# A masked-reconstruction loss: even columns to VectorE, odd ones to PE and ScalarE near the end, the target further forward in the stream, scales by pairs

One core of one Trainium2 chip. The metric is the device time of one execution in microseconds (us), least is best; the kernel before takes 77.78 us.

## The reference

```python
pred, target: (32, 147, 768) float32            # randn
mean = target.mean(-1, keepdims=True); var = target.var(-1, keepdims=True)
target = (target - mean) / np.sqrt(var + 1e-6)  # norm_pix_loss is True
loss = np.mean((pred - target) ** 2, axis=-1)
return loss.mean(axis=-1)                       # (32,)
```

## The kernel before

The 32 x 147 rows are laid on 128 partitions: each holds 36 or 37 rows, here called columns 0 to 36, of 768 elements (column 36, the rest, is on 96 partitions). `t` is target, `p` is pred. For each column VectorE makes mean and variance, ScalarE and VectorE the scale `r` and the negated mean `nm`, GpSimd the normalised column `s`. Then one of three ways: PE computes p - s into PSUM and ScalarE squares and sums it ("ACT"); VectorE takes the difference and ScalarE squares it ("DVE+ACT"); or VectorE does both ("DVE"). PE sums over partitions at the end, into `acc`.

```python
piece("t", 0, 4, q="hw"); piece("t", REST, REST + 1, q="hw")     # ... one statement a line in the kernel
...
piece("p", 4, 8)
piece("t", 20, 24)
piece("p", 8, 12)
piece("t", 24, 28)
piece("p", 12, 16)
piece("t", 28, 32)
piece("p", 16, 20)
piece("t", 32, 36)
...                                       # pred 20 to 31 by pairs, 32 to 34 singly, 35 in halves

def normalise(u, c):                      # GpSimd: reads the target tile in SBUF
    ...
    pin(nc.gpsimd.tensor_scalar(out=s[:n, so:so + D], in0=til[:n, o:o + D], scalar1=nm, scalar2=r,
                                op0=ALU.add, op1=ALU.mult))
def difference(u, d0, w):                 # VectorE: both inputs in SBUF
    ...
    pin(nc.vector.tensor_tensor(out=z[:, :w], in0=til[:, o:o + w], in1=s[:, so + d0:so + d0 + w],
                                op=ALU.subtract))
def square_dve(u, d0, w, dest):
    z = zs[u, d0][:, :w]
    pin(nc.vector.scalar_tensor_tensor(out=z, in0=z, scalar=1.0, in1=z, op0=ALU.mult, op1=ALU.mult,
                                       accum_out=dest))
...
finals.insert(0, ("rl_sum", rl_sum, mask, P))
for i, (need, vec, m, n) in enumerate(finals):   # PE: sums over partitions, [1, 32] each
    op(("final", i), "PE", 0.2, [need, "masks"], lambda v=vec, m=m, n=n: final(v, m, n), rank=90.0)
```

`op` lists an operation with an engine, a guessed duration and what it needs; a loop then sorts all of them by a simulated start time, and that is the program order on each engine. So each engine runs in a fixed order, and a change of one guess or need can move others.

## Time and profile before

| | before |
|---|---|
| time, median | 77.78 us (77.77 to 77.79) |
| profiled span | 76.0 us |
| busy: DMA row | full in slices 2 to 36 of 40 |
| busy: GpSimd, VectorE, ScalarE, PE | 71%, 69%, 41%, 39% of the span |
| HBM read | 28.90 MB, 380 GB/s over the span |

The shares of busy time average over the whole span; the end is set by what happens from 66 us on, which the prediction shows line by line.

### The profile page before, as it was taken

Reading aid. Unit: us, or ns where it says so; the run is one execution under the profiler, and the core shown is the slowest. Engines: PE = TensorE matmul, PEld = TensorE weight load, DVE = VectorE, ACT = ScalarE, POOL = GpSimd, SP = SyncE. Lnnn points to the kernel's source line nnn. Section 1 sums busy time; section 2 is a strip of 40 time slices with the busy share of each in tenths; the row PEclk is TensorE's granted clock in tenths of the full one; section 3 lists DMA queues with packets and bytes.
Section 4 is the critical chain, followed back from the end, with each engine's and each line's share of the span. In section 5 each row is a group of like instructions: output and inputs, shape, how many; then the busy total and the mean of one; then the engine's idle time right before and its main releaser. Section 6 shows DMA issues by size and latency. Waiting matters only on the chain.

```text
span 76.0 us, 535 instructions
## 1 busy us (share of the span) xinstructions
PE 29.5 (39%) x85; PEld 8.8 (12%) x86; DVE 52.3 (69%) x139; ACT 31.1 (41%) x61; POOL 54.0 (71%) x76
## 2 busy tenths in 40 slices
PE   0000000056898940679187708751642200004550
PEld 0000000011323300212031103110111000001020
DVE  0000499999999999927960896099429995499960
ACT  5100000400269501088019503940591669952960
POOL 4998205299998987598986898984488839994000
PEclk9999999999999999999965995699999555555555
DMA  0899999999999999999999999999999999999400
GB/s 0 213 420 310 251 228 236 210 220 213 210 217 217 213 214 217 217 210 213 217 217 217 213 215 217 210 220 210 220 199 212 210 215 210 216 200 201 61 0 0
DMA packets 3830, 15.41 MB, mean 203 GB/s; under 512 B 435, under 2 KB 1171, under 8 KB 3699
## 3 DMA queue, kind: packets, MB, share of 16 engines
q0 software_dynamic: 3568, 13.52, 88.2%
q1 hardware_dynamic: 258, 1.87, 6.8%
q14 instruction: 4, 0.02, 0.1%
HBM read 28.90 MB, written 0.00 MB: 380 GB/s over the span
## 4 chain that ended last, share of the span: by engine, by line
DMA 66%; DVE 21%; POOL 7%; issue 2%; PE 1%; ACT 0%; POOLq 0%; DVEq 0%; ACTq 0%
DMA t<-in_target_dram 49%; DMA p<-in_pred_dram 17%; DVE st L163 13%; POOL s L213 6%; DVE mv L164 3%; DVE zd L254 3%; DVE zd L249 2%; POOL p L113 1%; PE acc L307 1%; ACT r L187 0%; DVE r L193 0%; DVE ob L336 0%; POOLq L213 0%; DVEq L249 0%; ACTq L187 0%
## 5 line engine op out<-in xcount | busy, mean ns | idle before, releaser
L163 DVE BATCH_NORM_STATS2 st<-t 128x6 f32<-128x384 bf16 (+2 forms) x74 | 36.1, 530 | 14.2 <-DMA t<-in_target_dram 14.2
L213 POOL TENSOR_SCALAR s<-t,nm,r 128x768 bf16<-128x768 bf16 (+2 forms) x37 | 38.2, 1038 | 4.3 <-DVE r L193 2.2
L227 PE MATMUL z<-s,nident 128*128 128x512 bf16 (+3 forms) x36 | 13.8, 499 | 31.3 <-POOL s L213 26.9
L242 ACT ACTIVATE z<-z 128x1536 f32<-128x1536 f32 (+2 forms) x13 | 17.0, 1311 | 12.0 <-PE z L227 12.0
L227 PE MATMUL z<-p,ident 128*128 128x512 bf16 (+3 forms) x35 | 14.2, 548 | 12.2 <-DMA p<-in_pred_dram 12.0
L113 POOL DMA_DIRECT2D p<-in_pred_dram x17 | 9.6, 566 | 9.2 <-DMA t<-in_target_dram 4.3
L187 ACT ACTIVATE r<-mv,eps_t 128x4 f32<-128x4 f32 (+1 forms) x10 | 2.9, 293 | 26.8 <-DVE mv L164 26.1
L249 DVE TENSOR_TENSOR zd<-p,s 128x768 bf16<-128x768 bf16 (+1 forms) x9 | 7.3, 842 | 2.1 <-DMA p<-in_pred_dram 1.1
L242 ACT ACTIVATE zd<-zd 128x1536 bf16<-128x1536 bf16 (+1 forms) x6 | 7.6, 1264 | 2.8 <-DVE zd L249 2.8
L164 DVE BATCH_NORM_AGGREGATE mv<-st 128x2 f32<-128x12 f32 (+1 forms) x37 | 7.7, 209 | 1.3
L227 PEld LDWEIGHTS <-nident 128*128 128x128 bf16 (+1 forms) x37 | 3.4, 113 | 42.3 <-issue 23.0
L227 PEld LDWEIGHTS <-ident 128*128 128x128 bf16 (+1 forms) x37 | 4.8, 129 | 19.8 <-issue 18.5
L113 POOL DMA_DIRECT2D t<-in_target_dram x8 | 4.8, 622 | 1.0 <-POOLq L354 0.8
L193 DVE RECIPROCAL r<-r 128x4 f32<-128x4 f32 (+1 forms) x10 | 1.5, 148 | 2.8 <-ACT r L187 2.8
L254 DVE SCALAR_TENSOR_TENSOR zd<-zd 128x768 bf16<-128x768 bf16 x3 | 2.8, 949 | 0.0
L242 ACT ACTIVATION_READ_ACCUMULATOR z<-z 128x1 f32 (+1 forms) x13 | 2.4, 188 | 0.0
L188 ACT ACTIVATE nm<-mv 128x4 f32<-128x4 f32 (+1 forms) x10 | 1.9, 189 | 0.0
L187 ACT ACT_TABLE_LOAD x1 | 1.3, 1283 | 0.8 <-PEq L354 0.8
L307 PE MATMUL acc<-mask,rl 128*1 128x32 f32 x8 | 1.0, 229 | 0.7 <-ACT zd L242 0.4
L242 ACT ACTIVATION_READ_ACCUMULATOR zd<-zd 128x1 f32 x6 | 1.1, 186 | 0.0
L152 DVE MEMSET eps_t<- 128x1 f32 x1 | 0.1, 59 | 0.9 <-PEq L354 0.9
L307 PEld LDWEIGHTS acc<-mask,rl 128*1 128x1 f32 x8 | 0.4, 87 | 1.9 <-ACT zd L242 1.3
(25 smaller groups left out, 5.7 us busy)
## 6 DMA issues: line engine op xcount, KB each, us to landing
t<-in_target_dram POOLq DMA_DIRECT2D x8, 768.0 KB, 26.1
p<-in_pred_dram POOLq DMA_DIRECT2D x5, 768.0 KB, 26.4
p<-in_pred_dram POOLq DMA_DIRECT2D x6, 384.0 KB, 22.3
t<-in_target_dram SPq DMA_DIRECT2D x1, 1536.0 KB, 7.9
p<-in_pred_dram POOLq DMA_DIRECT2D x3, 192.0 KB, 12.8
t<-in_target_dram SPq DMA_DIRECT2D x1, 288.0 KB, 10.6
p<-in_pred_dram POOLq DMA_DIRECT2D x2, 96.0 KB, 9.8
p<-in_pred_dram POOLq DMA_DIRECT2D x1, 144.0 KB, 10.5
```

The source lines that it names most:

```text
L113: pin(eng.dma_start(out=til[:n], in_=src))
L163: pin(nc.vector.bn_stats(out=st[:n, j, :], in_=x))
L164: pin(nc.vector.bn_aggr(out=out, in_=st[:n, :len(parts)]))
L187: pin(nc.scalar.activation(out=r[:n], in_=mv[:n, :, 1], func=ACTF.Sqrt, bias=eps_t[:n], scale=1.0))
L188: pin(nc.scalar.activation(out=nm[:n], in_=mv[:n, :, 0], func=ACTF.Copy, scale=-1.0))
L193: pin(nc.vector.reciprocal(out=rs[g][:n], in_=rs[g][:n]))
L213: pin(nc.gpsimd.tensor_scalar(out=s[:n, so:so + D], in0=til[:n, o:o + D], scalar1=nm, scalar2=r, op0=ALU.add, op1=ALU.mult))
L227: pin(nc.tensor.matmul(z[:n, a:b], eye[:n, :n], src[:n, so + a:so + b], start=first, stop=not first))
L242: pin(nc.scalar.activation(out=z[:n, :w], in_=z[:n, :w], func=ACTF.Square, accum_out=dest[:n]))
L249: pin(nc.vector.tensor_tensor(out=z[:, :w], in0=til[:, o:o + w], in1=s[:, so + d0:so + d0 + w], op=ALU.subtract))
L254: pin(nc.vector.scalar_tensor_tensor(out=z, in0=z, scalar=1.0, in1=z, op0=ALU.mult, op1=ALU.mult, accum_out=dest))
L307: pin(nc.tensor.matmul(acc, vec[:n], m[:n], start=len(turn) == 1, stop=len(turn) == len(finals)))
```

## The change

Its intent: the statistics and normalised columns should be ready before their pred arrives, and from column 28 on VectorE (even columns) and PE with ScalarE (odd columns) should take turns, so that neither falls behind the stream.

```diff
     piece("t", 20, 24)
+    piece("t", 24, 28)
     piece("p", 8, 12)
-    piece("t", 24, 28)
+    piece("t", 28, 32)
     piece("p", 12, 16)
-    piece("t", 28, 32)
-    piece("p", 16, 20)
     piece("t", 32, 36)
-    for c in range(20, 24, 2):
-        piece("p", c, c + 2)
-    for c in range(24, 32, 2):
+    for c in range(16, 32, 2):
         piece("p", c, c + 2)
...
-    groups = [...] + [tuple(range(c, c + 4)) for c in range(4, KM, 4)]
-    units = [((c, c + 1), 0, D, "ACT" if c < 22 else "DVE+ACT") for c in range(0, KM - 4, 2)]
+    groups = [...] + [tuple(range(c, c + 4)) for c in range(4, 16, 4)]
+    groups += [(c, c + 1) for c in range(16, KM, 2)]
+    units = [((c, c + 1), 0, D, "ACT" if c < 18 else "DVE+ACT") for c in range(0, 24, 2)]
...
-    # 28 DVE, 29 DVE+ACT, (30, 31) DVE+ACT, 32 DVE, 33 DVE+ACT, 34 DVE   (summary of several lines)
+    units += [((24,), 0, D, "DVE"), ((25,), 0, D, "DVE+ACT"), ((26, 27), 0, D, "DVE+ACT")]
+    units += [((c,), 0, D, "ACT" if c % 2 else "DVE") for c in range(28, KM - 1)]
...
-    tail = 4
+    tail = 5
...
-    op("rl_sum", "DVE", 0.2, early_ops, lambda: pin(nc.vector.tensor_reduce(
-        out=rl_sum, in_=rl, axis=mybir.AxisListType.X, op=ALU.add)), rank=50.0)
+    def early_sum():
+        junk = singles.tile([P, n_early], F32, name="junk")
+        pin(nc.scalar.activation(out=junk, in_=rl, func=ACTF.Copy, accum_out=rl_sum))
+    op("rl_sum", "ACT", 0.4, early_ops, early_sum, rank=50.0)
```

The rest of the diff (a third queue that no piece uses, and the simulated start of ScalarE) adds no instruction. Columns 24 and 25, one pair before, become single columns, and VectorE now squares 24.

More of the change, by code (lines that the diff above doesn't have):

```diff
@@ L81 @@
     piece("p", KM - 1, KM, half, D)
-    groups = [tuple(range(0, 4)), (REST,)] + [tuple(range(c, c + 4)) for c in range(4, KM, 4)]
-    units = [((c, c + 1), 0, D, "ACT" if c < 22 else "DVE+ACT") for c in range(0, KM - 4, 2)]
+    groups = [tuple(range(0, 4)), (REST,)] + [tuple(range(c, c + 4)) for c in range(4, 16, 4)]
+    groups += [(c, c + 1) for c in range(16, KM, 2)]
+    units = [((c, c + 1), 0, D, "ACT" if c < 18 else "DVE+ACT") for c in range(0, 24, 2)]
     units.insert(2, ((REST,), 0, D, "ACT"))
-    units += [((KM - 4,), 0, D, "DVE"), ((KM - 3,), 0, D, "DVE+ACT"), ((KM - 2,), 0, D, "DVE"),
-              ((KM - 1,), 0, half, "ACT"), ((KM - 1,), half, D, "ACT")]
-    k = units.index(((KM - 8, KM - 7), 0, D, "DVE+ACT"))
-    units[k:k + 1] = [((KM - 8,), 0, D, "DVE"), ((KM - 7,), 0, D, "DVE+ACT")]
+    units += [((24,), 0, D, "DVE"), ((25,), 0, D, "DVE+ACT"), ((26, 27), 0, D, "DVE+ACT")]
+    units += [((c,), 0, D, "ACT" if c % 2 else "DVE") for c in range(28, KM - 1)]
+    units += [((KM - 1,), 0, half, "ACT"), ((KM - 1,), half, D, "ACT")]
     ops, by_name = [], {}
@@ L108, in load @@
         n, w = rows_of(c0), d1 - d0
-        til = data.tile([P, (c1 - c0) * w], F32 if q == "hw" else BF16, name=f"{kind}{c0}_{d0}")
+        til = data.tile([P, (c1 - c0) * w], BF16 if q == "sw" else F32, name=f"{kind}{c0}_{d0}")
         src = bass.AP(tensor=x.tensor, offset=x.offset + c0 * D + d0,
                       ap=[[N * D, B], [KJ * D, J - 1 if c0 == REST else J], [1, (c1 - c0) * w]])
-        eng = nc.sync if q == "hw" else nc.gpsimd
+        eng = {"hw": nc.sync, "hw2": nc.scalar, "sw": nc.gpsimd}[q]
         pin(eng.dma_start(out=til[:n], in_=src))
@@ L115, in load @@
             KIND[kind].setdefault(c, []).append((d0, d1, til, (c - c0) * w))
-    land, lanes, clock, last = {}, {"hw": [], "sw": []}, 2.9, {}
+    land, lanes, clock = {}, {"hw": [], "hw2": [], "sw": []}, 2.9
     for i, (kind, c0, c1, d0, d1, q) in enumerate(stream):
@@ L125 @@
         k = len(lanes[q])
-        op(("load", i), "SP" if q == "hw" else "POOL", 0.6, [], lambda a=stream[i]: load(*a), rank=-1.0,
+        op(("load", i), {"hw": "SP", "hw2": "ACT", "sw": "POOL"}[q], 0.6, [], lambda a=stream[i]: load(*a), rank=-1.0,
            early=0.0 if k <= 8 else lanes[q][k - 9] + 0.3)
@@ L314 @@
     free = {e: 0.0 for e in ("SP", "POOL", "DVE", "ACT", "PE")}
-    free["ACT"] = 2.1
+    free["ACT"] = 0.0
     end, left, order = {}, list(range(len(ops))), []
```

## The prediction

> **What bounds the kernel now.** I read the page first: the rows of 40 slices and the shares of the chain that ended last.
>
> ```profile
> DMA  0899999999999999999999999999999999999400
> GB/s 0 213 420 310 251 228 236 210 220 213 210 217 217 213 214 217 217 210 213 217 217 217 213 215 217 210 220 210 220 199 212 210 215 210 216 200 201 61 0 0
> DMA 66%; DVE 21%; POOL 7%; issue 2%; PE 1%; ACT 0%; POOLq 0%; DVEq 0%; ACTq 0%
> ```
>
> One slice is 1.9 us. The DMA row is full from slice 2 to slice 36, so for some 69 of the 76.0 us the queues had work without a gap. GB/s counts what is written, and most tiles are cast from f32 to bf16, so what is read is twice that, 28.90 MB in all. No engine sits above 71%. The stream is the bound, and the change removes no byte from it. All that is open to a change of order and of engines is the part after the stream, so the second view is the timeline of the last 13 us (start, length, engine, line, operation):
>
> ```profile
> 63.01 6.18 POOL L213 TENSOR_SCALAR s<-t,nm,r 128x768 bf16<-128x768 bf16 x4
> 66.22 1.41 DVE L249 TENSOR_TENSOR zd<-p,s 128x768 bf16<-128x768 bf16 x2 [1.11 <-DMA p<-in_pred_dram]
> 67.56 0.94 DVE L254 SCALAR_TENSOR_TENSOR zd<-zd 128x768 bf16<-128x768 bf16 x1
> 68.44 2.50 DVE L249 TENSOR_TENSOR zd<-p,s 128x1536 bf16<-128x1536 bf16 x3
> 70.86 0.94 DVE L254 SCALAR_TENSOR_TENSOR zd<-zd 128x768 bf16<-128x768 bf16 x1
> 71.12 0.48 PE L227 MATMUL z<-p,ident 128*128 128x384 bf16 x1 [1.08 <-DMA p<-in_pred_dram]
> ...
> 71.62 0.48 PE L227 MATMUL z_last<-p,ident 128*128 128x384 bf16 x1
> 71.73 0.08 DVE L254 DVE_READ_ACCUMULATOR zd<-zd 128x1 f32 x1
> 71.73 0.55 DVE L249 TENSOR_TENSOR zd<-p,s 128x768 bf16<-128x768 bf16 x1
> ...
> 72.32 0.96 DVE L254 SCALAR_TENSOR_TENSOR zd<-zd 128x768 bf16<-128x768 bf16 x1
> 72.34 0.47 ACT L242 ACTIVATE z<-z 128x384 f32<-128x384 f32 x1
> ...
> 72.84 0.47 ACT L242 ACTIVATE z_last<-z_last 128x384 f32<-128x384 f32 x1
> ...
> 73.20 0.17 DVE L300 TENSOR_REDUCE rl_sum<-rl 128x1 f32<-128x18 f32 x1
> ...
> 73.85 0.18 DVE L336 COPY ob<-acc 1x32 f32<-1x32 f32 x1 [0.49 <-PE acc L307]
> ```
>
> The two halves of the last column reach PE at 71.12 and 71.62, which I take as their landings. VectorE has no gap from 66.22 to 73.37: it enters the last 5 us behind the stream. Its columns 32 and 34 land before the last column, yet their squares end at 71.8 and 73.28. ScalarE, kept busy by the squares that follow VectorE's differences, takes up the first half at 72.34, though PE was done with it at about 71.60. Both engines end at about 73.4, so 1.8 us lie between the last landing and the last square. From there to `ob` it is 0.4 us, and 2.15 us more to the end of the span. The third view, the groups by shape in 61 to 76 us (busy us, mean ns), shows why VectorE is late:
>
> ```profile
> L213 POOL TENSOR_SCALAR s<-t,nm,r 128x768 bf16<-128x768 bf16 x4 | 6.2, 1557 | 0.0
> L249 DVE TENSOR_TENSOR zd<-p,s 128x1536 bf16<-128x1536 bf16 x4 | 4.4, 1112 | 1.0 <-POOL s L213 0.9
> L254 DVE SCALAR_TENSOR_TENSOR zd<-zd 128x768 bf16<-128x768 bf16 x3 | 2.8, 949 | 0.0
> ```
>
> GpSimd's last four normalisations take 1557 ns each, where the median of all 37 is 976 and the longest 2452; VectorE's longest difference of two columns takes 1561 ns where the median of the nine differences of either width is 919. Both are slow only while the other runs.
>
> **What the Trainium skill says.** "SBUF — State Buffer", Who interferes with whom: a VectorE instruction with two SBUF inputs contends with a GpSimd instruction that reads SBUF, and the later one waits for all of the earlier. The stretched pairs above agree. "VectorE: DVE Perf Modes", The perf-mode tier table: a bf16 `tensor_tensor` runs at twice the plain rate and has no faster form. The trace agrees as far as it goes: 0.55 us for 768 elements, 0.92 for 1536, against 0.95 for the `scalar_tensor_tensor` over 768. So a column's square costs VectorE far more than its difference. "DMA: Bandwidth & Descriptors", Bandwidth, gives rates for whole transfers; none is needed here, as this trace has the rate.
>
> **The change part by part.**
>
> *Engines from column 28 on.* VectorE before, from 28 to 34, counted from column 28's arrival: 1.41 (differences 28, 29), 0.95 with its accumulator read (square 28), 2.50 (differences of 30 with 31, 32 and 33, one of them stretched), 0.95, 0.55, 0.96, with small overlaps 66.22 to 73.28, 7.06 us. After: columns 28, 30, 32 and 34 alone, each a difference of 0.55 and a square with read of about 1.0, 4 x 1.55 = 6.2 us. From 66.2 that is 72.4 at the earliest. The stream sets no later end: taking a column as about 0.93 us of stream (the last landings before show that pace), pair 30 lands at about 67.7, column 32 at 68.7, and 34 at 70.6. VectorE then squares 30 by 69.3, 32 by 70.85 and 34 by 72.4. This saves 0.9 us there, of which 0.6 is the stretch that goes with GpSimd's late normalisations, the rest the three differences of odd columns less one square.
>
> ScalarE: odd columns need PE's two products (about 0.75 us after landing at the half clock that the trace grants from 58 us on) and a square of 768. I put that at 0.84, as for `zd`, plus 0.19 for the read, 0.95 with overlap. Column 31: landing 67.7, PE 68.5, square to 69.45. Column 33: landing about 69.6, PE 70.4, square to 71.4. So ScalarE is free when PE has the first half at 71.6: squares 71.65 to 72.2 and 72.2 to 72.75. Before, they were the same two instructions from 72.34 to 73.43, 1.09 us. They start 0.7 us earlier, no longer behind VectorE's backlog.
>
> *Target further forward.* In the listing of the stream, target pieces 24, 28 and 32 each move past one piece of four pred columns, so each lands 3.66 us sooner (the waits of `bn_stats` on target, at 41.96, 49.28 and 56.61, put eight columns at 7.32 us). Target 32 lands at 52.95 and its statistics take 4.6 us, to 57.6, where before they ended at 61.2. The last normalisations can then end by about 62, not 69.2, far before VectorE's tail. This removes the stretch from the tail; it takes nothing from the stream.
>
> *Scales by pairs.* From column 16 on, ten pairs in place of five groups of four: five more each of square root (0.29), negated mean (0.19) and reciprocal (0.15). That is 2.4 us on ScalarE and 0.75 on VectorE, all before 59 us, where VectorE waits some 2 us for each target piece. Cost on the path: nothing. Gain: GpSimd starts a pair 2.3 us sooner, also off the path.
>
> *Columns 18 to 21 to VectorE.* Two more differences of 1536, 1.84 us, at 57.6 to 60. VectorE catches up by the time pair 22 lands at about 60.3 and pair 24 at 62.2; these can still be stretched by GpSimd.
>
> *Early sums by ScalarE.* The `tensor_reduce` of 0.17 at 73.20 goes; ScalarE's sum of about 0.4 us falls between squares 31 and 33, at 69.5 to 69.9, where it waits only for pred. The path loses a reduction that sat on the end of VectorE; some of it was beside ScalarE's last square.
>
> *Pieces.* One pred piece of four columns (16 to 19) becomes two. One more issue of 0.55 on GpSimd, and perhaps 0.04 of stream.
>
> Sum: the path is last landing 71.6 (unchanged), PE 0.48, square and read to 72.75, then as before 0.4 to `ob` at 73.15 in place of 73.85. **Minus 0.7 us**, span 75.3. The timed median is 1.78 above the profiled span before, so 77.1.
>
> **The rivals.** *A: PE's order gives it back.* The listing of instructions shows PE taking the sums of columns into `acc` in between: the last half's product stands behind the sum of column 33, which needs ScalarE's square at 71.4, only 0.2 before the last landing. The subtraction for the last column's first half stands behind the square of 31. If PE or ScalarE is 0.4 late there, the tail is 0.3 to 0.4 longer: 77.4 to 77.5. For it: the granted clock of 0.5 and three engines in a ring. Against it: the slack above.
>
> *B: the stream gets longer.* GpSimd issues in order and an issue waits for the landing eight back, so a normalisation that waits for a pair's reciprocal, behind a square waiting for a later pred, could hold an issue. Then 0.3 to 1 us more, 77.4 to 78.5. Against: I followed each late issue through the order; the last needs pair 24's landing at 62.2, as before, 8 us ahead of its data.
>
> *C: the stream gets shorter.* From 66 us on the rate was 194 to 215 GB/s against a steady 215. If GpSimd's and VectorE's collisions cause that, their removal gives up to 0.3 us: 76.8. Against it: small pieces at the end explain it as well, and these stay. A gain of 2% needs 1.56 us, nearly the whole 1.8 us behind the last landing; I see no way to it.
>
> **Range and chances.** The middle is 77.1. C alone gives 76.8, A gives 77.5, and a mild B lies within; 76.75 to 77.5 should hold it 8 times in 10. Within 2% (76.22 to 79.34): 0.94. Faster than that needs stream and tail together: 0.04. Slower needs a hard form of B: 0.02.
>
> **What would show it.** Right: PE takes the last half at 71.5 to 71.7; ScalarE takes the first half within 0.1 us of PE's end; VectorE's last square ends near 72.4 and ScalarE's at 72.75; the last four normalisations end before 63; differences of 768 stay near 0.55; `ob` near 73.15. Wrong: the last landing moves by over 0.3 us (B or C); PE's last product starts later than its landing (A); a DMA share under 0.9 in any slice to 36; VectorE still without a gap at 72.5.

## The result

Ratios here and below are the mean time of one kernel's fast runs over the mean of the kernel before's in the same rounds, so not quite the ratio of the medians quoted beside them.

The changed kernel takes 77.25 us (77.17 to 77.32, six runs) against 77.80 in the same rounds: a ratio of 0.993 (0.9917 to 0.9943), and 0.55 us faster. The span went from 76.0 to 75.6 us. The page of the changed kernel, the same rows as before:

```profile
DMA  0799999999999999999999999999999999999700
GB/s 0 208 416 315 252 231 229 224 221 208 208 211 218 215 219 218 221 208 208 211 218 218 212 218 224 208 211 202 216 211 211 211 211 213 211 203 206 107 0 0
DMA 60%; DVE 18%; POOL 9%; issue 6%; PE 2%; ACT 1%; POOLq 0%; ACTq 0%
```

The stream is as full and as long as before; its last slice with data holds 107 GB/s in place of 61 because each slice is now 75.6/40 us. So nothing came from the transfers. The timeline of the changed kernel's tail (start, length, engine, line, operation, and in brackets the idle time ahead and who ended it) answers to the one in the prediction:

```profile
69.66 0.48 PE L224 MATMUL z<-s,nident 128*128 128x384 bf16 x1 [0.17 <-ACT z L239]
...
69.93 0.84 PE L224 MATMUL z<-p,ident 128*128 128x512 bf16 x2
...
70.81 0.80 ACT L239 ACTIVATE z<-z 128x768 f32<-128x768 f32 x1 [0.86 <-PE z L224]
...
71.22 0.48 PE L224 MATMUL z<-p,ident 128*128 128x384 bf16 x1 [0.26 <-DMA p<-in_pred_dram]
71.48 0.96 DVE L251 SCALAR_TENSOR_TENSOR zd<-zd 128x768 bf16<-128x768 bf16 x1
...
71.63 0.40 PE L307 MATMUL acc<-mask,rl 128*1 128x32 f32 x4
71.74 0.47 ACT L239 ACTIVATE z<-z 128x384 f32<-128x384 f32 x1
...
71.96 0.50 PE L224 MATMUL z_last<-p,ident 128*128 128x384 bf16 x1
...
72.50 0.47 ACT L239 ACTIVATE z_last<-z_last 128x384 f32<-128x384 f32 x1 [0.18 <-PE z_last L224]
...
73.44 0.18 DVE L336 COPY ob<-acc 1x32 f32<-1x32 f32 x1 [0.99 <-PE acc L307]
```

VectorE's last square now runs from 71.48 to 72.45, where it ended at 73.28. ScalarE takes the first half at 71.74, not at 72.34. `ob` comes at 73.44, not at 73.85, though the first half landed 0.1 us later in this trace (71.22 against 71.12, where PE stood idle for it). A measure free of that shift is the **tail**: from the start of the first half's pred product to `ob`. It was 73.85 - 71.12 = 2.73 us and is 2.22. That 0.5 is the gain.

Not all went well: the last half's product starts at 71.96, though in the kernel before it followed the first half's by 0.5 us (71.62 behind 71.12), so that the data should be there at about 71.7. Just ahead of it in PE's order stand four passes of sums (from 71.63): two for column 32, and two for column 33, and these two need ScalarE's square of 33, ended at 71.71. And GpSimd is later than I had reckoned. Here are its last normalisations, and VectorE's first difference, in order of time:

```profile
57.57 1.94 POOL L210 TENSOR_SCALAR s<-t,nm,r 128x768 bf16<-128x768 bf16 x2
57.62 2.69 DVE L246 TENSOR_TENSOR zd<-p,s 128x1536 bf16<-128x1536 bf16 x1
...
60.61 2.28 POOL L210 TENSOR_SCALAR s<-t,nm,r 128x768 bf16<-128x768 bf16 x1 [0.59 <-DVE r L190]
...
63.45 1.95 POOL L210 TENSOR_SCALAR s<-t,nm,r 128x768 bf16<-128x768 bf16 x1
```

A difference that takes 0.92 us alone lasted 2.69 us beside two normalisations, and held back the reciprocal behind it; the last two normalisations then stretched to 2.28 and 1.95 us. They end at 65.4 us, not at 62, but still ahead of the tail.

### The profile page after: what moved, and what is told of

Same layout as the page of the kernel before. It is cut to its first block, busy times and chain, and to the rows that moved or that the text cites. A ratio compares the mean times of both kernels' runs of the same rounds, so it can differ in the third digit from the quotient of the medians.

```text
span 75.6 us, 570 instructions
## 1 busy us (share of the span) xinstructions
PE 30.1 (40%) x87; PEld 8.9 (12%) x88; DVE 56.4 (75%) x148; ACT 32.0 (42%) x73; POOL 54.5 (72%) x77
## 2 busy tenths in 40 slices
DMA packets 3973, 15.41 MB, mean 204 GB/s; under 512 B 450, under 2 KB 1186, under 8 KB 3842
## 3 DMA queue, kind: packets, MB, share of 16 engines
HBM read 28.90 MB, written 0.00 MB: 382 GB/s over the span
## 4 chain that ended last, share of the span: by engine, by line
DMA 60%; DVE 18%; POOL 9%; issue 6%; PE 2%; ACT 1%; POOLq 0%; ACTq 0%
DMA t<-in_target_dram 49%; DVE st L160 13%; DMA p<-in_pred_dram 11%; POOL s L210 8%; DVE mv L161 3%; DVE zd L246 1%; PE acc L307 1%; POOL t L110 1%; PE z L224 1%; ACT z_last L239 1%; PE z_last L224 1%; POOLq L368 0%; DVE r L190 0%; POOL p L110 0%; DVE ob L336 0%
## 5 line engine op out<-in xcount | busy, mean ns | idle before, releaser
L224 PE MATMUL z<-s,nident 128*128 128x512 bf16 (+4 forms) x36 | 13.8, 493 | 23.1 <-POOL s L210 17.2
L239 ACT ACTIVATE z<-z 128x1536 f32<-128x1536 f32 (+3 forms) x14 | 16.6, 1184 | 7.6 <-PE z L224 7.3
L224 PE MATMUL z<-p,ident 128*128 128x512 bf16 (+4 forms) x35 | 14.8, 558 | 12.6 <-DMA p<-in_pred_dram 12.3
L184 ACT ACTIVATE r<-mv,eps_t 128x2 f32<-128x2 f32 (+2 forms) x15 | 4.4, 293 | 29.7 <-DVE mv L161 28.9
L110 POOL DMA_DIRECT2D p<-in_pred_dram x18 | 10.2, 566 | 3.2 <-DMA p<-in_pred_dram 2.2
L246 DVE TENSOR_TENSOR zd<-p,s 128x768 bf16<-128x768 bf16 (+1 forms) x10 | 9.7, 991 | 0.5 <-ACT zd L239 0.3
L239 ACT ACTIVATE zd<-zd 128x1536 bf16<-128x1536 bf16 (+1 forms) x5 | 6.7, 1346 | 2.7 <-DVE zd L246 2.7
L251 DVE SCALAR_TENSOR_TENSOR zd<-zd 128x768 bf16<-128x768 bf16 x5 | 4.8, 955 | 0.1
L190 DVE RECIPROCAL r<-r 128x2 f32<-128x2 f32 (+2 forms) x15 | 1.9, 124 | 2.2 <-ACT r L184 2.2
L185 ACT ACTIVATE nm<-mv 128x2 f32<-128x2 f32 (+2 forms) x15 | 2.8, 189 | 0.0
```

What stands on the lines that cost most here:

```text
L110: pin(eng.dma_start(out=til[:n], in_=src))
L184: pin(nc.scalar.activation(out=r[:n], in_=mv[:n, :, 1], func=ACTF.Sqrt, bias=eps_t[:n], scale=1.0))
L185: pin(nc.scalar.activation(out=nm[:n], in_=mv[:n, :, 0], func=ACTF.Copy, scale=-1.0))
L190: pin(nc.vector.reciprocal(out=rs[g][:n], in_=rs[g][:n]))
L224: pin(nc.tensor.matmul(z[:n, a:b], eye[:n, :n], src[:n, so + a:so + b], start=first, stop=not first))
L239: pin(nc.scalar.activation(out=z[:n, :w], in_=z[:n, :w], func=ACTF.Square, accum_out=dest[:n]))
```

## The experiments

The question is which part of the change brought the 0.5 us. **Theory E**: the swap of engines, which takes the odd columns off VectorE. **Theory C**: the order of the stream, which ends GpSimd's normalisations before VectorE's tail, so that the two no longer stretch each other. The prediction counted both in its 0.9 us for VectorE and divided them only by reckoning. All experiments gave correct results and were timed in five rounds, with four to six runs kept of each.

| run | median us | ratio to before (95%) | tail us |
|---|---|---|---|
| before | 77.7 to 77.8 | 1 | 2.73 |
| changed | 77.25 | 0.993 (0.9917 to 0.9943) | 2.22 |
| only_engines | 77.59 | 0.9987 (0.9974 to 1.0) | 2.70 |
| only_stream | 77.11 | 0.9932 (0.992 to 0.9944) | 2.12 |
| undo_engines | 77.13 | 0.9931 (0.9918 to 0.9945) | 2.15 |
| undo_stream | 78.36 | 1.0084 (1.0071 to 1.0096) | late start |
| undo_pairs | 77.99 | 1.0019 (1.0002 to 1.0037) | late start |
| undo_sum | 77.29 | 0.9943 (0.9931 to 0.9955) | 2.28 |
| extra_reads | 79.26 | 1.0202 (1.018 to 1.0224) | 4.10 |
| extra_writes | 77.24 | 0.994 (0.9928 to 0.9953) | 2.13 |
| sums_last | 77.02 | 0.9908 (0.9896 to 0.9921) | 1.96 |
| pe_order | 76.93 | 0.9903 (0.9889 to 0.9918) | 1.95 |
| pe_split | 77.27 | 0.9942 (0.9928 to 0.9955) | 2.04 |
| old_engines_sum | 77.15 | 0.9926 (0.9912 to 0.9939) | 2.11 |

"Late start" means that PE took the first half well after it landed, so the measure does not hold there. In pe_split the first piece is larger and lands later.

### One part alone, and the change without it

**only_engines**: the kernel before with

```diff
+    units += [((c,), 0, D, "ACT" if c % 2 else "DVE") for c in range(28, KM - 1)]
```

in place of its units from 28 to 34.

> The kernel before, with only the engines of columns 28 to 35 as in the changed kernel (even ones VectorE alone, odd ones PE and ScalarE). Theory E (the swap of engines does it: VectorE has 4 x 1.55 us in place of 7.06): 77.3 to 77.4, VectorE's last square at about 72.4 to 72.7. Theory C (the gain is the normalisations leaving the tail, so VectorE's two-input instructions are no longer stretched): the last normalisations still run to about 69 us and still stretch a difference, and the odd columns now wait for them on PE; 77.7 to 77.9, with a normalisation or a difference of over 1.5 us after 66 us.

At 77.59 us it lies in neither range, and is 0.1 us under the kernel before, at the edge of noise. The trace has the sign that was named for C: normalisations still ran past 66 us (to 67.97), and VectorE's square of 28 took 1.63 us and its difference 0.82. VectorE's last square ended at 73.19, hardly sooner than before. Its timeline:

```profile
62.96 5.01 POOL L209 TENSOR_SCALAR s<-t,nm,r 128x768 bf16<-128x768 bf16 x4
...
66.29 0.82 DVE L245 TENSOR_TENSOR zd<-p,s 128x768 bf16<-128x768 bf16 x1 [1.24 <-DMA p<-in_pred_dram]
...
67.15 1.63 DVE L250 SCALAR_TENSOR_TENSOR zd<-zd 128x768 bf16<-128x768 bf16 x1
```

**only_stream**: the kernel before with only the new order of pieces.

```diff
+    piece("t", 24, 28)
     piece("p", 8, 12)
...
+    for c in range(16, 32, 2):
```

> The kernel before, with only the order of the stream as in the changed kernel (target pieces 24, 28, 32 earlier, pred 16 to 19 as two pieces). Theory E: VectorE still has the differences of 29, 31, 33 in its tail; 77.6 to 77.8. Theory C: normalisations end by 63 us, the two-column difference of 30 and 31 falls from 1.56 to 0.95 us, VectorE's last square ends at about 72.7 in place of 73.3; 77.2 to 77.4.

This has the whole gain, 0.57 us (77.11, below both ranges), and a shorter tail than the changed kernel. The difference of columns 30 and 31 fell from 1.56 to 0.96 us. VectorE's last square ended at 72.68 in place of 73.28, and these 0.60 us are the size of the gain:

```profile
71.72 0.96 DVE L251 SCALAR_TENSOR_TENSOR zd<-zd 128x768 bf16<-128x768 bf16 x1
```

These are its groups by shape in 66 to 76 us (busy us, mean ns):

```profile
L251 DVE SCALAR_TENSOR_TENSOR zd<-zd 128x768 bf16<-128x768 bf16 x3 | 2.9, 951 | 0.0
...
L210 POOL TENSOR_SCALAR s<-t,nm,r 128x768 bf16<-128x768 bf16 x1 | 1.3, 1288 | 0.1
L246 DVE TENSOR_TENSOR zd<-p,s 128x1536 bf16<-128x1536 bf16 x1 | 1.0, 959 | 0.1
```

The one normalisation that reaches into the window began at 64.89 and was over by 66.2, later than the 63 that I expected.

**undo_engines**: the changed kernel with columns 28 to 34 on the engines of before.

> The changed kernel, with columns 28 to 34 on the engines of the kernel before. Theory E: gives the gain back, 77.6 to 77.8. Theory C: keeps most of it, 77.3 to 77.45, because the early sum on ScalarE and the early normalisations stay.

Taking the swap back costs nothing: 77.13, below both ranges and at the same ratio as the changed kernel. Theory E falls as the source of the gain. This kernel still has the early sum on ScalarE, the scales by pairs and the new engines of columns 18 to 21, 24 and 25, and only_stream has none of these. The two ratios are 0.9931 and 0.9932, so with the old engines from column 28 on, these parts together bring nothing that can be told from noise.

**undo_stream**: the changed kernel with the old order of pieces.

> The changed kernel, with the stream's order of the kernel before. Theory E: 77.3 to 77.4. Theory C: normalisations end near 69 us again, and hold PE's subtraction of columns 33 and 35; 77.6 to 77.9.

All of the change but the stream is slower than the kernel before, by 0.84%, beyond what C expected. The last two normalisations began at 64.27 and took 5.10 us together, beside VectorE's own work:

```profile
63.98 3.83 DVE L249 TENSOR_TENSOR zd<-p,s 128x1536 bf16<-128x1536 bf16 x5
...
64.27 5.10 POOL L213 TENSOR_SCALAR s<-t,nm,r 128x768 bf16<-128x768 bf16 x2 [0.59 <-DVE r L193]
...
69.42 0.48 PE L227 MATMUL z_last<-s,nident 128*128 128x384 bf16 x1 [2.60 <-POOL s L213]
69.69 0.84 PE L227 MATMUL z<-p,ident 128*128 128x512 bf16 x2
```

The harm comes through PE's order: the subtraction for the last half needs the last normalised column and stands in PE's order ahead of column 31's product. PE waited 2.60 us for it while column 31's pred lay ready, as the product took off at once behind it. The swap by itself does not do this: only_engines has the same order on PE, but its normalisations ended at 67.97, not at 69.37, PE waited 0.98 us, and it was no slower than the kernel before. Which of the other parts made the normalisations later no run separates.

### The contention by itself

**extra_reads**: only_stream with four normalisations into a tile that nobody reads, behind GpSimd's last needed one. They add no need to any other engine, so what is put back is only GpSimd's reading of SBUF beside VectorE.

```diff
+    def extra():
+        x = singles.tile([P, 2 * D], BF16, name="x")
+        for j in range(4):
+            til, r = tbuf[KM - 1][0][2], rs[KM - 1]
+            pin(nc.gpsimd.tensor_scalar(out=x[:, 0:D], in0=til[:, j * D:(j + 1) * D], scalar1=r[1], scalar2=r[0],
+                                        op0=ALU.add, op1=ALU.mult))
+    op("extra", "POOL", 4.0, [("norm", KM - 1)], extra, rank=80.0)
```

> The stream-order-only kernel (77.11) with four more normalisations into a scratch tile, nobody's input, at the end of GpSimd's order, so that they run from 66 us on beside VectorE's tail as the needed ones did in the kernel before. Contention theory: some of VectorE's instructions of 0.55 and 0.95 us there stretch to 1.0 us and more, and the time is 0.3 to 0.8 us longer, 77.4 to 77.9. Rival (the gain was in having the normalised columns sooner, not in a free port): unchanged, 77.05 to 77.2.

79.26 us: 2.1 us more than only_stream, and well over the upper end of what I expected. Each of VectorE's three squares in the tail took 1.5 to 1.6 us (two are shown):

```profile
65.97 7.88 POOL L301 TENSOR_SCALAR x<-t,nm,r 128x768 bf16<-128x768 bf16 x4
...
66.94 1.57 DVE L251 SCALAR_TENSOR_TENSOR zd<-zd 128x768 bf16<-128x768 bf16 x1
...
73.11 1.54 DVE L251 SCALAR_TENSOR_TENSOR zd<-zd 128x768 bf16<-128x768 bf16 x1
```

This shows the mechanism and not its size. The extra normalisations run to 73.85, where the needed ones of the kernel before ended at 69.19; there the differences were stretched (1.41 and 2.50 us above) and the squares kept 0.94 us.

**extra_writes**: the control, with six memsets of 768 bf16 in the same place.

```diff
-            pin(nc.gpsimd.tensor_scalar(...))
+            pin(nc.gpsimd.memset(x[:, 0:D], 0.0))
+            if j < 2:
+                pin(nc.gpsimd.memset(x[:, D:2 * D], 0.0))
```

> The control to extra_reads: six memsets of 768 bf16 in the same place, which write SBUF and read nothing. Contention over the reading side only: VectorE's instructions keep 0.55 and 0.95 us and the time stays at 77.05 to 77.2. If any GpSimd work in the tail costs: 77.3 or more.

77.24 us, 0.04 above the range given, with an interval that overlaps only_stream's and the same tail within 0.01 us. The square that runs beside memsets kept its 0.95 us; the other two come after the last memset, which ended at 70.29. The differences beside them took 1.03 and 1.43 us, where only_stream has 1.08 and 1.43:

```profile
66.73 0.73 POOL L302 MEMSET x<- 128x768 bf16 x1
67.03 0.95 DVE L251 SCALAR_TENSOR_TENSOR zd<-zd 128x768 bf16<-128x768 bf16 x1
```

So GpSimd's normalisations, which read SBUF, stretch VectorE's instructions with two inputs, and are stretched in turn (1.56 to 2.33 us each in extra_reads, 0.98 alone); GpSimd's being busy is not enough. VectorE's instructions with one input show nothing of it: the 74 `bn_stats` of the kernel before, many of them beside normalisations, took 503 to 562 ns. Theory C is shown: the mechanism by these two runs, its size by only_stream.

### The other parts

**undo_pairs**: the changed kernel with

```diff
-    groups = [...] + [tuple(range(c, c + 4)) for c in range(4, 16, 4)]
-    groups += [(c, c + 1) for c in range(16, KM, 2)]
+    groups = [...] + [tuple(range(c, c + 4)) for c in range(4, KM, 4)]
```

> The changed kernel with scales of columns 16 to 35 by fours again. Theory: off the path; the last normalisations end at 66 to 68 us in place of 65.4, if that reaches past 66 us one square of VectorE stretches by 0.3 to 0.6 us, and VectorE has slack of 0.3 only: 77.2 to 77.6. Rival: pairs cost VectorE and ScalarE time that shows: 77.0 to 77.15.

77.99 us (77.64 to 78.05, a wide scatter), over the range given, and no faster than the kernel before. The normalisation of 32 waits for the statistics of all four columns and starts at 59.73, not 57.57; the last ends at 67.45, not 65.4. That stretches the square of 28, as expected, and does what I had not seen: PE's subtraction for the last half, which needs that last column, holds the products of 29 and 31 behind it.

```profile
66.71 1.54 DVE L250 SCALAR_TENSOR_TENSOR zd<-zd 128x768 bf16<-128x768 bf16 x1
67.50 0.48 PE L223 MATMUL z_last<-s,nident 128*128 128x384 bf16 x1 [8.04 <-POOL s L209]
...
67.77 1.49 PE L223 MATMUL z<-p,ident 128*128 128x512 bf16 x4
```

In the changed kernel the product of 29 started at 66.01. So beside the rest of the change the pairs are needful, where only_stream, with scales by fours as well, is at 77.11. The trace points to the swap, which puts 29 and 31 on PE; no run has fours with the swap and the new stream alone.

**undo_sum**: the early sum on VectorE again, by a `tensor_reduce` at the end of its order.

> The changed kernel with the early sum by VectorE again, at the end of its order. VectorE ends at 72.45 + 0.17 = 72.62, ScalarE's last square at 73.08, so the sum is hidden: 77.2 to 77.3. Rival: it sits on the path: 77.35 to 77.45.

77.29, hidden: VectorE made the sum at 72.42, while ScalarE's last square was still to come (72.61).

### PE's order

**sums_last**: the changed kernel, with every sum but the first two needing (in the sorting only) the last product.

```diff
-    op(("final", i), "PE", 0.2, [need, "masks"], lambda ...)
+    op(("final", i), "PE", 0.2, [need, "masks"] + ([("pred", len(units) - 1)] if i > 1 else []), lambda ...)
```

> One half of pe_order: only the sums of columns 32 and 33 go behind the last half's product; the subtraction for the last column's first half still stands ahead of column 33's pred product. If the place of the sums is the whole loss: 76.9 to 77.0, as pe_order. If the subtraction's place matters as much, ScalarE still ends column 33 at 71.7 and takes the first half at 71.75: 77.0 to 77.15.

77.02 us: the last product started 0.50 us behind the first half's and `ob` came 0.26 us sooner. The place of the sums is nearly the whole loss. By the ratios it is 0.17 us, and the intervals just touch; the tails, one trace of each, say 0.26.

```profile
71.72 0.48 PE L224 MATMUL z_last<-p,ident 128*128 128x384 bf16 x1
```

**pe_order**: the same, and the subtraction for the last column's first half behind column 33's product.

```diff
-    ... + ["ident"],
+    ... + ["ident"] + ([("pred", k - 2)] if (u, d0) == ((KM - 1,), 0) else []),
```

> The changed kernel with PE's order alone altered: column 33's pred product ahead of the subtraction for the last column's first half, and the sums of columns 32 and 33 behind the last half's product. Theory Q (the changed kernel loses 0.3 us in PE's queue: the last half, landed by about 71.65, is taken up at 71.96): the last product starts within 0.1 us of its landing, 0.2 to 0.35 us faster than the changed kernel measured 77.25, so 76.9 to 77.05. Rival: VectorE's square of column 34 ends at 72.45 and ScalarE is as full as PE, so nothing is gained: 77.2 to 77.3.

76.93 us, the fastest of all, 0.32 us under the changed kernel's median (0.21 us by the ratios, each taken against the kernel before in its own rounds). The second step is not told apart from sums_last (0.9903 and 0.9908, tails 1.95 and 1.96). PE in its tail:

```profile
71.13 0.48 PE L224 MATMUL z<-p,ident 128*128 128x384 bf16 x1
71.62 0.48 PE L224 MATMUL z_last<-p,ident 128*128 128x384 bf16 x1
72.03 1.01 PE L307 MATMUL acc<-mask,rl 128*1 128x32 f32 x10
```

**pe_split**: pe_order, with the last column cut at 512 in place of 384.

> As pe_order, and the last column is cut at 512 of 768 in place of 384. Theory Q with a shorter last piece: its product and its square are over a third shorter, 0.15 us less than pe_order, 76.75 to 76.95, unless VectorE's square of 34 (72.45) or the first piece's longer square then ends last: no change against pe_order.

A miss: 77.27. The first piece reached PE 0.26 us later than in pe_order's trace and its product and square are longer, so ScalarE took it up at 72.00 and began the last at 72.59, where pe_order's began at 72.14. Of the two cuts tried, equal halves are the better: there ScalarE begins the last square as soon as it has done with the first.

**old_engines_sum**: undo_engines, with ScalarE's early sum moved ahead of its last two squares, to see whether the swap is worth something once PE's order is good.

```diff
-    op(("sq", k), "ACT", ..., [("pred", k)], ...)
+    op(("sq", k), "ACT", ..., [("pred", k)] + (["rl_sum"] if u == (KM - 1,) else []), ...)
```

> undo_engines (ratio 0.9931) with ScalarE's early sum moved from behind the last square to ahead of the last column's two squares; PE's order there has no sum ahead of the last product. Theory: the swap of engines is worth something only where PE's order is good: this kernel loses 0.13 to 0.2 us against undo_engines and still ends with VectorE's square of 34 at 72.6, so 77.0, above pe_order (ratio 0.9903) by under 0.1. Rival: the swap is worth nothing or less: equal to pe_order or faster, a ratio of 0.990 or under.

77.15, not 77.0, a miss: the tail is 2.11 against undo_engines' 2.15, because VectorE's square of 34 ended at 72.85 and three sums came after it. pe_order's tail is 0.16 shorter, with that square ended at 72.35. The intervals of the two ratios overlap slightly (0.9889 to 0.9918, 0.9912 to 0.9939), so where nothing waits in PE's order the swap is worth 0.16 us by the traces, one of each, and 0.18 by the ratios, not clear of noise. In the changed kernel PE's order took it back.

## Why the prediction was right, and where its steps failed

The forecast of 77.1 in 76.75 to 77.5 held: 77.25. The stream stayed and the gain came from VectorE's end, as forecast. That the median came within 0.15 us is in part luck: `ob` was 0.3 us later than forecast (73.44 against 73.15), but the difference of median and profiled span was 1.65 us, not the 1.78 taken from before, where the profiled execution had itself been 0.07 us under the median (77.71). Of the signs named, VectorE's end and ScalarE's taking the first half at once (71.74) held; the last half's start, ScalarE's end (72.97 for 72.75), the normalisations' end and `ob` did not. By its own steps:

- **The stream's end does not move.** Right: the first half reached PE at 71.22 against 71.12. Rivals B and C of the prediction did not happen. One reading was loose: 28.90 MB read is 1.9 times the 15.41 MB written, not twice, as some pieces stay f32.
- **VectorE ends at 72.4.** Right: 72.45, with differences of 552 ns on average. Of its 0.9 us it gave 0.6 to the stretch, and the new stream alone brought 0.57. It gave 0.3 to the swap of engines, and this did not come: the runs give the swap alone about 0.1 us, at the edge of noise, and nothing beside the new stream (undo_engines). Its reading of the lines left out that the differences of 28 and 29 were stretched too (1.41 us, against 1.08 in only_stream).
- **Columns 18 to 21 to VectorE.** Wrong in the cost: of the 1.84 us for two differences, the first alone took 2.69 (57.62 to 60.31). VectorE had caught up at 62.35, where it waits for pred again. No run undoes this part by itself.
- **Normalisations end by about 62.** Wrong: 65.4, though the statistics ended at 57.7 as forecast. The step let differences and normalisations run beside each other from 57.6 on at their own lengths, with a remark that they could be stretched; one difference took 2.69 us, and the reciprocals behind it came late. No effect on the time shows: in the tail VectorE had a gap of 0.27 us at 67.95.
- **Scales by pairs: no gain on the path.** Wrong: without them the changed kernel is 0.9% slower (1.0019 over 0.993), as the last normalised column then holds PE's order and VectorE's square.
- **The early sum.** Near enough: it left VectorE and took ScalarE 0.3 us in a gap (69.64 to 69.94). undo_sum shows that the gain is not told from none.
- **PE, and the sum of 0.7 us.** The sum came out at 0.41 in the traces and 0.55 in the medians. Of the missing 0.3, the first half's later start is 0.1; the rest is rival A, for which the text gave 0.3 to 0.4: the product that the text put right behind the last landing started at 71.96 behind the sums of columns 32 and 33. The slack of 0.2 that I held against it was not there, because column 33's product started at 69.93, behind a subtraction that waited for ScalarE, and its square ended at 71.71, not 71.4. How much of the delay is this wait, and how much the passes themselves, no run separates.

## What to carry to other kernels

In a kernel bound by its transfers, look at what lies between the last landing and the end, and then at which engines stretch each other there: moving GpSimd's reading work ahead of VectorE's last two-input instructions was worth all of the gain here, and moving work between engines without that was worth 0.1 us, at the edge of noise. An engine with a fixed order pays for each small instruction that stands ahead of the one the end waits for: two small sums (four passes), moved behind the last product, shortened the tail by 0.26 us, nearly all that reordering gave. Undo each part of a composite change by itself, for a part that seems to bring nothing can be what another part needs.

## What the Trainium skill lacked or had wrong

- "SBUF — State Buffer", Who interferes with whom, says that the later of the two waits until the earlier is done. It does not say what happens with a queue behind: here a difference that started at 57.62 lasted 2.69 us, 1.77 more than alone, through two normalisations that ran from 57.57 to 59.51, so it was passed over once more. And four normalisations and VectorE's squares alternated in extra_reads, where a square went from 0.95 to 1.57 us and a normalisation from 0.98 to between 1.56 and 2.33.
- The same section names `tensor_tensor` as its example. The runs show it for `scalar_tensor_tensor` with one tile as both inputs too (0.95 to 1.57 us), and agree that a GpSimd instruction that only writes does no harm (0.95 us beside memsets).
- Small matmuls have their own costs in the pages, but none of the pages says what f32 sums that wait for another engine cost ahead of an awaited product; here four f32 passes of 32 columns, two of them waiting for ScalarE, delayed the last product by about 0.25 us (71.96 against 71.72 in sums_last, with the first half at 71.22 in both).
